# Attention values in one tile per head pair, with rows at places modulo 16

## The chip, the cores and the metric

The kernel runs on one core of one Trainium2 chip. The metric is the device time of one execution in microseconds, the median of several runs. Five engines work side by side: PE (TensorE, with its weight loads shown as PEld), DVE (VectorE), ACT (ScalarE), POOL (GpSimd) and SP (SyncE, which here only issues DMAs). Each engine takes its own instructions in order; semaphores tie them together.

## The reference

One layer of an encoder over 2048 tokens of width 1024 in float32. The tokens form a grid of 32 rows of 64. The tokens are normalised, projected to q, k, v and a gate for 16 heads of 64, and each token attends to a neighbourhood of 8 rows by 16 columns around it, with a learned bias:

```python
def row_fn(r):
    rs = jnp.clip(r - kh // 2, 0, rows - kh)          # kh = 8 key rows
    kr = lax.dynamic_slice_in_dim(kg, rs, kh, axis=1)[:, :, col_idx]
    vr = lax.dynamic_slice_in_dim(vg, rs, kh, axis=1)[:, :, col_idx]
    s = jnp.einsum('bnqhd,bknjhd->bhnqkj', qr, kr) * scale
    s = jnp.where(col_valid[None, None], s + bias[None], NEG_INF)
    p = jax.nn.softmax(s.reshape(B, H, nb, NA_QBLOCK, kh * NA_KBLOCK), axis=-1)
    o = jnp.einsum('bhnqkj,bknjhd->bnqhd', p, vr)
...
x = x + (o * jax.nn.silu(gate)) @ w_out
return rmsnorm(x, norm_f)
```

## The kernel before, in words

The first 561 us are the two projection stages (`stage_one`, `stage_two`), the last 120 us the output product and the final norm. Between them lies the attention stage, which the change touches.

Attention is done in 32 cycles. A cycle m is one entry of `order`: a pair of heads p (8 pairs; s = 0, 1 tells the two heads apart) and a frame T. A frame is 8 query rows and the key rows that they see; T = 0, 1, 2, 3 go down the grid. Cycles 0 to 15 take T = 1, then T = 0 for each pair; cycles 16 to 27 take T = 2, then T = 3 for pairs 0 to 5; cycles 28 to 31 are (6, 2), (7, 2), (7, 3), (6, 3). So a pair has a first run (T = 1 or 2) and a second run (T = 0 or 3) that share the key tile `KT`.

A frame's queries are cut in two halves of 4 rows, and its 64 columns in two quads of 4 groups of 8 columns. `HALF_ROWS[T][half]` says at which row of the frame a half's keys begin and how many rows they are (8 or 11). `FRAME[T]` is the grid row at which the frame begins, `TALL` the number of rows that the values' tile holds, 15. A tile `X[quad, half, s]` has 3 blocks of 8 columns for each of these rows, 3 x 8 x 15 = 360 elements per partition.

The loop body for cycle m runs, in program order:

- `begin(m)`: puts the coming loads on a list that is worked off while PE counts on (`later_loads`): the gate of cycle m-1, bias, queries and keys of cycle m+1 (`load_bias`, `load_q`, `load_k`) and the values of cycle m (`load_v`, L1265). All of them are issued by SP's queue, in order.
- feeds of other PE work, some 13.5 products of 128x512 (about 3 us): the last projections (L384 to L388) at first, output products (L1614 to L1618) later. Their weights and rows are split in two parts on ACT and DVE (`consume` with L185/L186 or L190/L191, `split_og` with L1455/L1456) before the turns.
- `normalise` of the quad left over from the cycle before: a reciprocal of the sums on DVE (L1357) and the scaling of X, by POOL (L1362) except for quad 1, half 1, which ACT (L1364, s = 1) and DVE (L1366, s = 0) scale.
- `turns(m-1)`: 48 transposes (L1382) of `8 * TALL` columns of X into six PSUM banks, copied to `pta` by ACT (L1389) and DVE (L1387), three copies each. Then `clear_x` has POOL zero those rows of X that the next frame does not write (L1316).
- `scores(2m)` and `scores(2m+1)`: 64 products (L1331), on DVE the sum with the bias and its minimum (L1342), on ACT the exponential with its sum (L1350), one per quad, half and s: 8 in a cycle.
- `values(m-1)`: 36 products (L1407) over `8 * TALL` partitions of `pta` and the values' tile; the product with the gate (L1413); its store (L1416).

The values of cycle m come as one DMA of 15 rows (120 partitions of 4 KB) into a tile of its own; the pool `vp` has two buffers. The keys of a first run come as one DMA (15 rows and 8 columns, or 16 rows), and those of a second run as one DMA of four rows into the same tile.

Of the kernel before, what the change touches and what calls it, by code (L numbers as in the profile page):

```python
# [11 lines left out]
F32 = mybir.dt.float32  # L12
# [3 lines left out]
AF = mybir.ActivationFunctionType  # L16
OP = mybir.AluOpType
# [44 lines left out]
def build(ctx, tc, x, xr, xt, wg, bias, w_out, n0, nf, out):  # L62
# [1167 lines left out]
            tc.add_manual_dep(d.ins, marks[at].ins.name, mybir.DependencyInfo(mybir.DependencyClass.Sync, mybir.DependencyReason.DATA),  # L1230
                              reason="loads spread over the run")

    def load_k(p, T):
        r0, r1, more = PARTS[T]
        base = 12 * (T > 1)
        a, b = r0 * GW, r1 * GW + more
        must(*[("k", p, c) for c in range(a // 512, (b + 511) // 512)])

        def keys():
            if T in (1, 2):  # L1240
# [3 lines left out]
            if T == 2:  # L1244
                nc.gpsimd.memset(t[:, 1280:1288], 0.0)
            not_until(nc.sync.dma_start(t[:, a - base * GW:b - base * GW], kd[p][:, a:b]), "values")

        return keys

    def load_q(p, T):  # L1250
        must(("q", p, T))

        def queries():
            QT[p, T] = qp([128, 512], F32, "q")
            nc.sync.dma_start(QT[p, T], qd[p][T])

        return queries

    def load_v(p, T):
        r0, r1 = FRAME[T], FRAME[T] + TALL  # L1260
        must(*[("v", p // 4, t) for t in range(r0 // 2, (r1 + 1) // 2)])
        rows = vd[p // 4][p % 4][r0 * 8192:r1 * 8192].rearrange("(k x) -> k x", x=1024)
        t = vp([128, 1024], F32, "vt")
        VT[p, T] = t.rearrange("p (s d) -> p s d", s=8)
        nc.sync.dma_start(t[:8 * TALL], rows)  # L1265

    def load_sg(p, T):
        must(("g", p, T))
# [27 lines left out]
    def make_x():  # L1296
        for half in range(2):
            for quad in range(2):
                for s in range(2):
                    X[quad, half, s] = t = xp([128, 512], F32, f"x{s}")[:, :24 * TALL]  # L1300
                    nc.gpsimd.memset(t, 0.0)
            t = ep([128, 528], F32, "sums")
            nc.gpsimd.memset(t, -NEG)
            sums.extend((t[:, :264], t[:, 264:]))
            held[half] = HALF_ROWS[order[0][1]][half]

    def clear_x(T):
        stale = []
        for half in range(2):
            (u0, n0), (u1, n1) = held[half], HALF_ROWS[T][half]  # L1310
            held[half] = u1, n1
            stale += [(half, a, b - a) for a, b in ((u0, min(u0 + n0, u1)), (max(u0, u1 + n1), u0 + n0)) if a < b]
        for quad in range(2):
            for half, a, n in stale:
                for s in range(2):
                    nc.gpsimd.memset(by_strip(X[quad, half, s], (a, n)), 0.0)  # L1316

    def scores(i, between=None):
        p, T, quad = pairs[i]
        kt, qt = KT[p, T // 2], QT[p, T]  # L1320
        both = [bank(512, f"s{s}") for s in range(2)]
        places = {}
        for half, (u, n) in enumerate(HALF_ROWS[T]):
            for s in range(2):
                places[half, s] = both[s][:, 256 * half:256 * half + WIDE * n]
            for h in range(4):
                g = 4 * quad + h
                for s in range(2):
                    a = slice(s * 64, s * 64 + 64)
                    o = (FRAME[T] + u - 12 * (T > 1)) * GW + 8 * FIRST[g]  # L1330
                    product = nc.tensor.matmul(places[half, s][h * 32:h * 32 + 32], qt[a, g * 64 + half * 32:g * 64 + half * 32 + 32],  # L1331
                                               kt[a, o:o + n * GW].rearrange("p (r c) -> p r c", c=GW)[:, :, :WIDE],
                                               start=True, stop=True, skip_group_check=True)
        if quad == 0:
            marks["scored"] = product
        ST[i] = st = tiny.tile([128, 12], F32, name="st")
        for half, (u, n) in enumerate(HALF_ROWS[T]):
            table = EM[p, T // 2, kinds_of[T][half]][quad]
            rows = [t[:, :24 * n].rearrange("p (r c) -> p r c", c=24) for t in sums[2 * half:2 * half + 2]]
            for s in range(2):  # L1340
                o = 2 * half + s
                nc.vector.tensor_tensor_reduce(rows[s][:, :, :WIDE], places[half, s].rearrange("p (r c) -> p r c", c=WIDE),  # L1342
                                               table[s].rearrange("p (r c) -> p r c", c=WIDE), -1.0, 1e38,
                                               OP.add, OP.min, st[:, o:o + 1])
            if between and half == 0:
                between()
            for s in range(2):
                o = 2 * half + s
                to = by_strip(X[quad, half, s], HALF_ROWS[T][half]).rearrange("p b (r c) -> p b r c", c=8)
                nc.scalar.activation(to, rows[s].rearrange("p r (b c) -> p b r c", b=3), AF.Exp, bias=st[:, o:o + 1], scale=-1.0,  # L1350
                                     accum_out=st[:, 4 + o:5 + o])

    def normalise(i, half):
        st = ST[i]
        _, T, quad = pairs[i]
        o = 2 * half
        nc.vector.reciprocal(st[:, 8 + o:10 + o], st[:, 4 + o:6 + o])  # L1357
        for s in range(2):
            f = st[:, 8 + o + s:9 + o + s]
            t = by_strip(X[quad, half, s], HALF_ROWS[T][half])  # L1360
            if quad == 0 or half == 0:
                nc.gpsimd.tensor_scalar(t, t, f, 1.0, op0=OP.mult, op1=OP.mult)  # L1362
            elif s:
                nc.scalar.activation(t, t, AF.Copy, scale=f)  # L1364
            else:
                nc.vector.tensor_scalar(t, t, f, None, op0=OP.mult)  # L1366
# [27 lines left out]
    def values(m):  # L1394
        p, T = order[m]
        k = 8 * TALL
        o = bank(512, "o")
        vt = VT[p, T]
# [12 lines left out]
        del VT[p, T]  # L1411
        og = ev([128, 512], F32, "og")
        nc.vector.tensor_tensor(og, o, SG.pop((p, T)), OP.mult)  # L1413

# [403 lines left out]
    def begin(m):  # L1818
# [113 lines left out]
```

## Time and profile before

| | |
|---|---|
| median of 3 runs | 992.08 us (988.28 to 993.48) |
| the profiled execution: time, span | 992.66 us, 990.9 us |
| granted PE clock, mean | 0.997 |
| busy: PE, PEld, DVE, ACT, POOL | 979.0, 796.7, 753.9, 531.9, 161.2 us |
| attention stage | 561 to 869 us of the span |
| moved by DMA | 227.95 MB |
| issues of values, of keys | 32, 32 |
| DMA to landing, values (480 KB), median | 5.9 us |

A timeline row gives start and length of a stretch in us, the engine and line, the operation, out<-in by the program's names, shapes, how many instructions were merged, and in brackets how long the engine idled before and what it waited for. A row of the groups gives count, busy us, mean ns of one, and the idle time before them with what ended it. "Issue" is idle time for which the profile shows no reason.

### The profile page before, as it was taken

What the parts mean: (1) busy time and instruction counts of PE and PEld (TensorE: products, weight loads), DVE (VectorE), ACT (ScalarE), POOL (GpSimd) and SP (SyncE); (2) the same over time, 40 slices, a digit from 0 to 9 for tenths busy, and PEclk for the clock granted to TensorE, in tenths of its full rate; (3) what the DMA queues carried; (4) which work ended last, traced back from release to release, by engine and by line L of the source; (5) the groups of instructions that cost most, each with busy time, mean ns of one, the idle gap of its engine ahead of it and who ended that gap; (6) DMA issues with size and microseconds to landing.
All of it is one profiled execution on the core that took longest, in us unless ns stands there. A gap on an engine that the chain in (4) does not pass through costs nothing.

```text
span 990.9 us, 22736 instructions
## 1 busy us (share of the span) xinstructions
PE 979.0 (99%) x8172; PEld 796.7 (80%) x8172; DVE 753.9 (76%) x1735; ACT 531.9 (54%) x1310; POOL 161.2 (16%) x430
## 2 busy tenths in 40 slices
PE   9999999999999999999999999999999999999996
PEld 6888888888888888888888778777778787888885
DVE  6899888988565876766775677768868888877865
ACT  7873245465535342343433477678768777653442
POOL 0000001231100000000001134334343343312110
PEclk9999999999999999999999999999999999999998
DMA  8943548777957836657465799988989988797753
GB/s 294 327 133 101 197 128 256 248 243 248 374 156 225 279 112 200 193 181 228 161 182 196 245 296 292 270 243 258 310 271 293 284 243 264 235 381 195 213 141 108
DMA packets 149970, 227.95 MB, mean 230 GB/s; under 512 B 13536, under 2 KB 66016, under 8 KB 149856
## 3 DMA queue, kind: packets, MB, share of 16 engines
q1 hardware_dynamic: 146832, 221.37, 70.9%
q0 software_dynamic: 2592, 4.72, 2.8%
q8 instruction: 65, 1.06, 0.4%
q14 instruction: 49, 0.40, 0.1%
q10 hardware_dynamic: 432, 0.40, 0.1%
HBM read 160.37 MB, written 66.06 MB: 229 GB/s over the span
## 4 chain that ended last, share of the span: by engine, by line
PE 98%; DMA 0%; issue 0%; ACT 0%; DVE 0%; ACTq 0%
PE pp L446 40%; PE pv L612 13%; PE py L1709 12%; PE o L1407 8%; PE s L1331 6%; PE ph L1382 5%; PE pp L388 2%; PE pp L384 2%; PE pp L386 2%; PE pv L727 2%; PE po L1618 2%; PE po L1614 2%; PE po L1616 2%; DMA raw<-in_wg_dram 0%; PE prb L235 0%
## 5 line engine op out<-in xcount | busy, mean ns | idle before, releaser
L446 PE MATMUL pp<-h,f 128*128 128x512 f32 x576 | 185.3, 389 | 0.0
L446 PE MATMUL pp<-t,f 128*128 128x512 f32 x702 | 171.3, 389 | 0.0
L446 PEld LDWEIGHTS pp<-t,f 128*128 128x128 f32 x702 | 131.8, 188 | 27.3
L1350 ACT ACTIVATE x<-sums,st 128x264 f32<-128x264 f32 (+1 forms) x256 | 124.5, 488 | 30.0 <-DVE st L1342 30.0
L446 PEld LDWEIGHTS pp<-h,f 128*128 128x128 f32 x576 | 108.1, 188 | 22.6
L446 PE MATMUL pp<-l,f 128*128 128x512 f32 x288 | 112.0, 389 | 0.0
L1362 POOL TENSOR_SCALAR x<-x,st 128x264 f32<-128x264 f32 (+1 forms) x192 | 89.0, 480 | 111.2 <-DVE st L1357 91.5
L1342 DVE CUSTOM_DVE_ANT_0 sums<-s,em 128x253 f32<-128x253 f32 (+1 forms) x256 | 91.1, 401 | 5.7 <-ACT x L1350 1.2
L429 DVE TENSOR_TENSOR f<-raw,f 128x512 fp32r<-128x512 f32 x105 | 75.9, 727 | 20.0 <-ACT f L428 19.8
L1407 PEld LDWEIGHTS o<-pta,vt 120*64 120x64 f32 x1152 | 69.9, 137 | 21.9 <-issue 15.1
L1407 PE MATMUL o<-pta,vt 120*64 120x192 f32 (+2 forms) x1152 | 84.6, 300 | 2.9 <-issue 2.9
L428 ACT ACTIVATE f<-raw 128x512 fp32r<-128x512 f32 x105 | 63.6, 622 | 36.6 <-DVE raw L435 22.0
L1387 DVE COPY pta<-ph 120x512 f32<-120x512 f32 x96 | 60.4, 684 | 16.5 <-PE ph L1382 16.3
L1389 ACT ACTIVATE pta<-ph 120x512 f32<-120x512 f32 x96 | 50.5, 599 | 35.9 <-PE ph L1382 35.9
L446 PEld LDWEIGHTS pp<-l,f 128*128 128x128 f32 x288 | 54.1, 188 | 11.2
L1331 PE MATMUL s<-kt,q 64*32 64x253 f32 (+1 forms) x2048 | 59.1, 362 | 0.0
L1382 PEld LDWEIGHTS ph<-ident,x 64*120 64x120 f32 x1536 | 47.6, 135 | 11.3 <-issue 10.6
L612 PE MATMUL pv<-wh,t 128*128 128x512 f32 x176 | 56.2, 389 | 0.0
L1709 PE MATMUL py<-woh,f 128*128 128x512 f32 x168 | 55.4, 390 | 0.0
L467 POOL TENSOR_TENSOR tmp<-tmp,rb 128x512 f32<-128x512 f32 x18 | 29.3, 1632 | 156.9 <-DVE tmp L464 141.1
L446 PE MATMUL pp<-sixths,f 128*128 128x512 f32 x198 | 52.7, 389 | 0.0
L1382 PE MATMUL ph<-ident,x 64*120 64x64 f32 x1536 | 52.0, 221 | 0.0
(231 smaller groups left out, 1888.3 us busy)
## 6 DMA issues: line engine op xcount, KB each, us to landing
raw<-in_wg_dram SPq DMA_DIRECT2D x124, 256.0 KB, 4.8
vt<-vd SPq DMA_DIRECT2D x32, 480.0 KB, 5.9
row<-in_xr_dram SPq DMA_DIRECT2D x32, 256.0 KB, 5.7
vd<-v SPq DMA_DIRECT2D x32, 256.0 KB, 3.3
sgd<-sg SPq DMA_DIRECT2D x32, 256.0 KB, 3.8
q<-qd SPq DMA_DIRECT2D x32, 256.0 KB, 4.0
sgt<-sgd SPq DMA_DIRECT2D x32, 256.0 KB, 4.7
ogd<-og SPq DMA_DIRECT2D x32, 256.0 KB, 5.9
```

Of the source, the lines that this page charges most:

```text
L428: nc.scalar.activation(t[:, 0], src, AF.Copy)
L429: nc.vector.tensor_tensor(t[:, 1], src, t[:, 0].bitcast(F32), OP.subtract)
L446: nc.tensor.matmul(B[n, P], t[:, int(m == 2), c], x[k][int(m == 1)], start=P in (1, 6, 5) and k == 0 and m == 0, stop=k == 3 and m == 2, s ...
L612: nc.tensor.matmul(p, a[:, o], b, start=P in (1, 6, 5) and k == 0 and m == 0, stop=k == 3 and m == 2, skip_group_check=True)
L1331: product = nc.tensor.matmul(places[half, s][h * 32:h * 32 + 32], qt[a, g * 64 + half * 32:g * 64 + half * 32 + 32], kt[a, o:o + n * GW].r ...
L1342: nc.vector.tensor_tensor_reduce(rows[s][:, :, :WIDE], places[half, s].rearrange("p (r c) -> p r c", c=WIDE), table[s].rearrange("p (r c) ...
L1350: nc.scalar.activation(to, rows[s].rearrange("p r (b c) -> p b r c", b=3), AF.Exp, bias=st[:, o:o + 1], scale=-1.0, accum_out=st[:, 4 + o: ...
L1362: nc.gpsimd.tensor_scalar(t, t, f, 1.0, op0=OP.mult, op1=OP.mult)
L1382: one_turn = nc.tensor.transpose(ph[h][:k, o:o + 64], X[quad, half, s][q, at:at + k], ident[q, q])
L1387: nc.vector.tensor_copy(o, i_)
L1407: product = nc.tensor.matmul(o[s * 64:s * 64 + 64, g0 * 64:g1 * 64], vt[:k, strip, s * 64:s * 64 + 64], moving, start=strip == 0, stop=str ...
L1709: nc.tensor.matmul(B[m, P], t[:, a, c], b, start=P in (1, 6, 5) and k == 0 and i == 0, stop=k == 3 and i == 2, skip_group_check=True)
```

## The change

`TALL` becomes 16, and a row r of the grid lies at place r modulo 16 in X, in `pta` and in the values' tile. The two runs of a pair share one values' tile: the first run's 16 rows are loaded as 12 and 4, the 12 one cycle earlier; the second run loads the four rows that differ over those that have become free (rows 0 to 3 for T = 0, 28 to 31 for T = 3), one cycle ahead of their use. The last four cycles, whose pairs cross, have exceptions. The keys of a first run come in two parts, the first 8 rows one cycle earlier.

Because of the modulus a half's rows may lie in two stretches: half 1 of T = 1 (places 8 to 15 and 0 to 2) and half 0 of T = 2 (places 12 to 15 and 0 to 6). There `scores` issues two exponentials instead of one, `normalise` adds the two sums on DVE and scales all 384 elements of the tile. `clear_x` works on sets of places. Turns and values span 128 columns and partitions instead of 120.

```diff
-FRAME, TALL = [0, 4, 12, 17], 15
+FRAME, TALL = [0, 4, 12, 17], 16
...
-    def load_k(p, T):
+    def load_k(p, T, part=None):
         r0, r1, more = PARTS[T]
         base = 12 * (T > 1)
-        a, b = r0 * GW, r1 * GW + more
+        first, last = part in (None, 0), part in (None, 1)
+        a = r0 * GW if first else (r0 + 8) * GW
+        b = r1 * GW + more if last else (r0 + 8) * GW
...
+    def keys_of(n):
+        (p, T), fs = order[n], []
+        if T not in (1, 2) or not in_parts(n):
+            fs.append(load_k(p, T))
+        else:
+            fs.append(load_k(p, T, 1))
+        if n + 1 < cycles and in_parts(n + 1):
+            fs.append(load_k(*order[n + 1], 0))
+        return fs
+
+    def in_parts(n):
+        return n > 1 and order[n][1] in (1, 2) and order[n - 1][1] in (0, 3)
...
-    def load_v(p, T):
-        r0, r1 = FRAME[T], FRAME[T] + TALL
+    def value_rows(n, r0, r1):
+        p, T = order[n]
         must(*[("v", p // 4, t) for t in range(r0 // 2, (r1 + 1) // 2)])
-        rows = vd[p // 4][p % 4][r0 * 8192:r1 * 8192].rearrange("(k x) -> k x", x=1024)
-        t = vp([128, 1024], F32, "vt")
-        VT[p, T] = t.rearrange("p (s d) -> p s d", s=8)
-        nc.sync.dma_start(t[:8 * TALL], rows)
+        o = r0 % TALL * 8
+        nc.sync.dma_start(VT[n][o:o + 8 * (r1 - r0)], vd[p // 4][p % 4][r0 * 8192:r1 * 8192].rearrange("(k x) -> k x", x=1024))
+
+    def first_values(n):
+        VT[n] = vp([128, 1024], F32, "vt")
+        value_rows(n, *{1: (4, 16), 2: (16, 28), 3: (16, 32)}[order[n][1]])
+
+    def load_values(m):
+        fs = []
+        if m and m - 1 < cycles - 1 and order[m - 1][1] in (0, 3):
+            VT[m - 1] = VT[m - 2]
+            fs.append(lambda: value_rows(m - 1, *((0, 4) if order[m - 1][1] == 0 else (28, 32))))
+        if m < cycles and order[m][1] in (1, 2):
+            if not in_parts(m):
+                fs.append(lambda: first_values(m))
+            fs.append(lambda: value_rows(m, *((16, 20) if order[m][1] == 1 else (12, 16))))
+        if m == cycles - 1:
+            fs.append(lambda: first_values(m))
+        elif m + 1 < cycles and in_parts(m + 1):
+            fs.append(lambda: first_values(m + 1))
+        return fs
...
+    def places_of(T, half):
+        u, n = HALF_ROWS[T][half]
+        return [(FRAME[T] + u + r) % TALL for r in range(n)]
+
+    def stretches(rows):
+        rows = list(rows)
+        cuts = [0] + [i for i in range(1, len(rows)) if rows[i] != rows[i - 1] + 1] + [len(rows)]
+        return [(a, rows[a], b - a) for a, b in zip(cuts, cuts[1:]) if a < b]
...
         stale = []
         for half in range(2):
-            (u0, n0), (u1, n1) = held[half], HALF_ROWS[T][half]
-            held[half] = u1, n1
-            stale += [(half, a, b - a) for a, b in ((u0, min(u0 + n0, u1)), (max(u0, u1 + n1), u0 + n0)) if a < b]
+            now_held = set(places_of(T, half))
+            stale += [(half, a, n) for _, a, n in stretches(sorted(held[half] - now_held))]
+            held[half] = now_held
...
-                to = by_strip(X[quad, half, s], HALF_ROWS[T][half]).rearrange("p b (r c) -> p b r c", c=8)
-                nc.scalar.activation(to, rows[s].rearrange("p r (b c) -> p b r c", b=3), AF.Exp, bias=st[:, o:o + 1], scale=-1.0,
-                                     accum_out=st[:, 4 + o:5 + o])
+                for k, (a, at, n_) in enumerate(stretches(places_of(T, half))):
+                    to = by_strip(X[quad, half, s], (at, n_)).rearrange("p b (r c) -> p b r c", c=8)
+                    e = 12 + s if k else 4 + o
+                    nc.scalar.activation(to, rows[s][:, a:a + n_].rearrange("p r (b c) -> p b r c", b=3), AF.Exp, bias=st[:, o:o + 1], scale=-1.0,
+                                         accum_out=st[:, e:e + 1])
...
+        places = stretches(places_of(T, half))
+        if len(places) > 1:
+            nc.vector.tensor_tensor(st[:, 4 + o:6 + o], st[:, 4 + o:6 + o], st[:, 12:14], OP.add)
         nc.vector.reciprocal(st[:, 8 + o:10 + o], st[:, 4 + o:6 + o])
         for s in range(2):
             f = st[:, 8 + o + s:9 + o + s]
-            t = by_strip(X[quad, half, s], HALF_ROWS[T][half])
+            t = X[quad, half, s] if len(places) > 1 else by_strip(X[quad, half, s], places[0][1:])
...
-            fs += [load_q(*nx), load_k(*nx)]
-        if m < cycles:
-            fs.append(lambda: load_v(*order[m]))
+            fs += [load_q(*nx), *keys_of(m + 1)]
+        fs += load_values(m)
```

More of the change, by code (lines that the diff above doesn't have):

```diff
@@ L1231, in not_until @@
                               reason="loads spread over the run")
-    def load_k(p, T):
+    def load_k(p, T, part=None):
         r0, r1, more = PARTS[T]
         base = 12 * (T > 1)
-        a, b = r0 * GW, r1 * GW + more
+        first, last = part in (None, 0), part in (None, 1)
+        a = r0 * GW if first else (r0 + 8) * GW
+        b = r1 * GW + more if last else (r0 + 8) * GW
         must(*[("k", p, c) for c in range(a // 512, (b + 511) // 512)])
         def keys():
-            if T in (1, 2):
+            if T in (1, 2) and first:
                 khalf.clear()
@@ L1243, in keys @@
             t = KT[p, T // 2]
-            if T == 2:
+            if T == 2 and last:
                 nc.gpsimd.memset(t[:, 1280:1288], 0.0)
@@ L1304, in make_x @@
             sums.extend((t[:, :264], t[:, 264:]))
-            held[half] = HALF_ROWS[order[0][1]][half]
+            held[half] = set(places_of(order[0][1], half))
     def clear_x(T):
@@ L1335, in scores @@
             marks["scored"] = product
-        ST[i] = st = tiny.tile([128, 12], F32, name="st")
+        ST[i] = st = tiny.tile([128, 14], F32, name="st")
         for half, (u, n) in enumerate(HALF_ROWS[T]):
@@ L1397, in values @@
         o = bank(512, "o")
-        vt = VT[p, T]
+        vt = VT[m].rearrange("p (s d) -> p s d", s=8)
         t = PT.pop(m)
```

1 line of the change is left out of this document (removed).

## The prediction

> **What bounds the kernel now.** I read the page's shares and its chain of work first, then the busy times of the attention stage alone, then the timeline of single cycles. Durations are from the profiled execution, 992.66 us with a span of 990.9 us, which stands 0.58 us above the median of the three runs, 992.08 us.
>
> ```profile
> span 990.9 us, 22736 instructions
> PE 979.0 (99%) x8172; PEld 796.7 (80%) x8172; DVE 753.9 (76%) x1735; ACT 531.9 (54%) x1310; POOL 161.2 (16%) x430
> ...
> PE 98%; DMA 0%; issue 0%; ACT 0%; DVE 0%; ACTq 0%
> ```
> ```profile
> 561.00:869.00 308.00, 305.07 (x5214) 241.60 (x5213) 242.25 (x883) 225.47 (x707) 111.01 (x378) 1.00 0.90 271
> ```
>
> PE is busy 99% of the span and is 98% of the chain. The second fence is the stage that the change touches (us of the stretch, then busy PE, PEld, DVE, ACT, POOL, granted clock, DMA share, GB/s): PE 305.07 of 308.00 us at the full clock, with the DMA engines 90% busy. So nothing can be gained there except by shorter PE work or by the 3 us in which PE idles, and what other engines lose costs nothing until PE waits for it. One cycle shows how far off such a wait is. This is cycle 12 (pair 6, frame 1), with other rows left out:
>
> ```profile
> 683.44 0.50 ACT L1350 ACTIVATE x<-sums,st 128x264 f32<-128x264 f32 x1
> ...
> 684.07 0.17 DVE L1357 RECIPROCAL st<-st 128x2 f32<-128x2 f32 x1 [0.54 <-ACT x L1350]
> 684.27 0.52 ACT L1364 ACTIVATE x<-x,st 128x264 f32<-128x264 f32 x1 [0.23 <-DVE st L1357]
> 684.34 0.48 DVE L1366 TENSOR_SCALAR x<-x,st 128x264 f32<-128x264 f32 x1
> 684.69 1.14 ACT L190 ACTIVATE woh<-raw 128x512 fp32r<-128x512 f32 x2
> 685.34 1.29 DVE L191 TENSOR_TENSOR wol<-raw,woh 128x512 fp32r<-128x512 f32 x2 [0.52 <-ACT woh L190]
> 685.82 1.49 PEld L1382 LDWEIGHTS ph<-ident,x 64*120 64x120 f32 x48 [0.35 <-issue]
> 685.82 1.62 PE L1382 MATMUL ph<-ident,x 64*120 64x64 f32 x48
> 686.54 1.58 ACT L1389 ACTIVATE pta<-ph 120x512 f32<-120x512 f32 x3 [0.71 <-PE ph L1382]
> 686.58 1.89 DVE L1387 COPY pta<-ph 120x512 f32<-120x512 f32 x3
> ...
> 687.38 1.71 PE L1331 MATMUL s<-kt,q 64*32 64x184 f32 x64
> ...
> 689.01 0.66 PE L1407 MATMUL o<-pta,vt 120*64 120x128 f32 x8
> ```
>
> The last exponential ends at 683.94. Behind it hang the reciprocal, the scaling of the probabilities (L1364 on ACT, L1366 on DVE), the weight split in the same queues (L190, L191), the turns on PE (L1382, from 685.82), their copies out of PSUM (L1389, L1387) and the values (L1407). Two margins are to be read. The last scaling ends at 684.82 and is first needed by the 13th of 48 turns, 12 x 1.49 / 48 = 0.37 us after 685.82: 1.4 us. DVE's copies end at 688.47 and the values begin at 689.01: 0.54 us.
>
> **The change part by part.** Prices by operation, from the groups by shape:
>
> ```profile
> L1350 ACT ACTIVATE x<-sums,st 128x264 f32<-128x264 f32 x192 | 96.3, 503 | 23.6 <-DVE st L1342 23.6
> L1350 ACT ACTIVATE x<-sums,st 128x192 f32<-128x192 f32 x64 | 28.3, 442 | 6.4 <-DVE st L1342 6.4
> L1357 DVE RECIPROCAL st<-st 128x2 f32<-128x2 f32 x128 | 20.2, 160 | 11.7 <-ACT x L1350 11.7
> L1364 ACT ACTIVATE x<-x,st 128x264 f32<-128x264 f32 x24 | 12.3, 514 | 5.3 <-DVE st L1357 5.3
> L1364 ACT ACTIVATE x<-x,st 128x192 f32<-128x192 f32 x8 | 3.6, 454 | 3.9 <-DVE st L1357 3.9
> L1362 POOL TENSOR_SCALAR x<-x,st 128x264 f32<-128x264 f32 x144 | 69.4, 497 | 91.5 <-DVE st L1357 91.5
> L1362 POOL TENSOR_SCALAR x<-x,st 128x192 f32<-128x192 f32 x48 | 19.9, 428 | 19.7 <-ACT x L1350 19.6
> L1316 POOL MEMSET x<- 128x72 f32 (+1 forms) x176 | 20.1, 166 | 75.7 <-PE ph L1382 75.2 <-POOL x L1316 0.5
> L1382 PE MATMUL ph<-ident,x 64*120 64x64 f32 x1536 | 52.0, 221 | 0.0
> L1382 PEld LDWEIGHTS ph<-ident,x 64*120 64x120 f32 x1536 | 47.6, 135 | 11.3 <-issue 10.6
> L1407 PEld LDWEIGHTS o<-pta,vt 120*64 120x64 f32 x1152 | 69.9, 137 | 21.9 <-issue 15.1 <-ACT x L1350 0.4 <-ACT pta L1389 0.4
> ```
>
> *Cut exponentials.* With row r at place r modulo 16, frame 1's half 1 (rows 8 to 18) and frame 2's half 0 (rows 12 to 22) wrap, the others do not. These are cycles 0, 2, ..., 28 and 29: 16 cycles, in each of which 2 quads x 2 heads exponentials become two, 64 more in all. 72 elements fewer save 503 - 442 = 61 ns, so one of 72 costs about 442 - 102 = 340 ns, and 192 + 72 cost 442 + 340 - 503 = 0.28 us more than 264 (96 + 168 the same, the price being a straight line). Exponentials follow each other without a gap, so the last of a cut cycle ends 4 x 0.28 = 1.12 us later. For frame 1 the sum of the two parts (a DVE operation on 128x2, taken at the reciprocal's 0.16 us) and the longer scaling over all 384 places (120 elements more, 0.10 us by L1364's two rows) are added: 1.38 us. For frame 2 those fall on half 0, which POOL scales, and the last scaling is 1.12 us late.
>
> *What that delay does.* In cycle 12 the last scaling ends 684.82 + 1.38 = 686.20, against 686.19 needed: the turns just hold. L190 and L191 move with it; L191 ends at 688.01 instead of 686.63, DVE's three copies follow it and end 1.89 us later at 689.90, and the values wait 0.89 us past 689.01. Behind the waiting values stand the next feed of projections and everything else on PE, so this is lost outright. Other cut cycles, with the turns' start and the values 3.19 us behind it as in cycle 12 (689.01 - 685.82):
>
> ```profile
> 611.81 0.69 DVE L186 TENSOR_TENSOR w<-raw,w 128x512 fp32r<-128x512 f32 x1 [0.66 <-ACT w L185]
> ...
> 612.16 0.96 PEld L1382 LDWEIGHTS ph<-ident,x 64*120 64x120 f32 x30 [0.35 <-issue]
> ...
> 647.71 0.47 DVE L1366 TENSOR_SCALAR x<-x,st 128x264 f32<-128x264 f32 x1
> ...
> 648.73 0.90 PEld L1382 LDWEIGHTS ph<-ident,x 64*120 64x120 f32 x27 [0.35 <-issue]
> ...
> 779.27 1.29 DVE L191 TENSOR_TENSOR wol<-raw,woh 128x512 fp32r<-128x512 f32 x2 [0.87 <-ACT woh L190]
> ...
> 779.54 0.84 PEld L1382 LDWEIGHTS ph<-ident,x 64*120 64x120 f32 x26 [0.35 <-issue]
> ```
>
> Cycle 22 (frame 2, two splits): L191 ends 780.56 + 1.12 = 781.68, the copies 783.57, values due 782.73: 0.84 us. Cycle 4 (one split): 612.50 + 1.38 + 1.89 = 615.77 against 615.35: 0.42 us. Cycle 8 (no split, little feed behind the exponentials): scaling 648.18 + 1.38 = 649.56 against 648.73 + 0.37 = 649.10: 0.46 us. So: cycles with two splits ahead of the turns (12, 14, 22, and 20 taken at 0.5) 3.1 us; with one item late on DVE (4, 6, 24, 26, 29) 5 x 0.4 = 2.0 us; cycle 8 and cycle 0 (0.3) 0.8 us; 2, 10, 16, 18 and 28 none, their queues having room. Sum 5.9 us. Bounds: nothing, if the queues' idle time takes it all; 16 x 1.38 = 22 us, if none does. I stay near the rows of single cycles.
>
> *Turns with 128 columns instead of 120* (and products over 128 rows instead of 120). A load of 64 columns takes 137 ns and one of 120 takes 135, so 8 columns more show nothing: 0. Upper end: the 48 loads of a cycle take 1.49 us, and if they set the pace, 8/120 of it for 32 cycles is 3.2 us. Lower end: the scores (L1331 in the fence of cycle 12) run 64 products in 1.71 us, 26.7 ns each against 1.62 / 48 = 33.8; at that pace the turns would gain 10.9 us.
>
> The Trainium skill, "TensorE: Matmul & The Clock Gate", section "LDWEIGHTS (loading the stationary operand)", has a load's time proportional to its columns, columns / 1.2 ns. By that, 8 columns are 6.7 ns, 10.2 us over 1536 loads if none were hidden, and the sum would be 1009. The trace does not agree in this kernel: 120 columns load no slower than 64.
>
> *POOL.* Clears go from 176 to 256 (0.166 us each), and 48 scalings grow from 264 to 384 elements (0.115 us each by L1362's two rows), some 19 us on an engine busy 16%. The clears run behind the turns while PE scores and DVE reduces; quad 0 is cleared first, and its exponentials come first. A scaling of half 0 that ends 0.2 us later is still needed only by the ninth turn. 0, at most 1 us.
>
> *Loads.* Values go from 32 issues of 480 KB (15 rows of 32 KB, 15.4 MB) to 48 (20 rows for each of 15 pairs, 32 for the one whose second run comes last, 10.6 MB), 4.7 MB less, keys go from 32 issues to 46. SP issues 30 more, about 1 per cycle; the release each waits for (the values two cycles back) is the one that L1265 waits for now. The new hazard: the four rows of a second run are loaded one cycle ahead, not two.
>
> ```profile
> 582.66 0.34 SPq L1265 DMA_DIRECT2D vt<-vd  x1
> ...
> 586.70 2.07 PE L1407 MATMUL o<-pta,vt 120*64 120x128 f32 x28
> ...
> kt<-kd SPq DMA_DIRECT2D x16, 128.0 KB, 3.9
> ```
> ```profile
> 727.69 2.56 PE L1407 MATMUL o<-pta,vt 120*64 120x128 f32 x34 [1.45 <-issue]
> ```
>
> The tightest is cycle 1: that issue slot at 582.66, values at 586.70, 4.0 us; a load of the same 128 KB takes 3.9 in the median. I take 0.4 us (0 to 3). Elsewhere the distance is about 6.5 us. Fewer bytes buy nothing: PE's idle time inside the stage, such as the 1.45 us of the last row, is put down to nothing that the profile shows, not to data. I leave it as it is (up to 3 us either way, if its place shifts).
>
> Sum: 992.66 + 5.9 + 0 + 0 + 0.4 = 999.0 us, 0.7% above the median.
>
> **The rivals.**
>
> *The cover holds (not slower).* The mechanism: the values need DVE's copies later than I charge, and the cut costs less than the straight line says. The first products of the values read columns that ACT's copies wrote (done at 688.12), DVE's are first read some four products on, 0.3 us. And queues with the idle time of cycle 12 (0.54 us before the copies' wait) absorb a delay of up to 0.5 us; that is 0.12 us for each cut instead of 0.28. From there down nothing is lost: 993. For it: PE's own waits for ACT and POOL at L1382 and L1407 are under 1 us in all now. Against: ACT's exponentials have no gaps, and cycle 12's DVE goes from L191 straight to the copies.
>
> *The turns run faster.* 128 columns is the full width, and the pace falls to that of the scores: 999.0 - 10.9 = 988, and with the cover holding 982, the only way to faster. Against: loads of 64 and 120 columns do not differ.
>
> *The loads set the turns' pace:* 999.0 + 3.2 = 1002. For it: PEld is busy 1.49 of the 1.62 us.
>
> *The late four rows:* 999.0 + 3 = 1002, if that part lands behind the rest of the queue. For it: DMA at 90%.
>
> **How the numbers follow.** Forecast 0.50 (996 to 1002), the loads' pace 0.08, late rows 0.05, cover holds 0.29 (992 to 995), faster turns 0.08. A measurement here tells about 0.5% from no change: slower begins at 997.0, faster ends at 987.1. Slower: the first three hold 0.63, less the part of the forecast that lies under 997, 0.08: 0.55. Faster: the faster turns, nearly always with some of the cover: 0.07. Same: the rest, 0.38. The time is 999.0; the range takes in the cover holding and both rivals at 1002, and leaves out the faster turns: 991 to 1004.
>
> **What would show it.** Exponentials 256 to 320, with ACT busy about 18 us more. PE waiting at the values for the copies, 0.4 to 0.9 us in cycles 4, 6, 12, 14, 20, 22, 24, with the longer waits where two splits stand ahead of the turns; at the turns in cycle 8. The turns' loads at 135 ns and 48 in 1.62 us. MB moved down by 4.7. Wrong it is if a cut exponential costs the ACT queue well under 0.28 us, if PE's idle time in the stage stays at 3 us, or if the turns' 1.62 us moves.

## The result and the profile after

The changed kernel takes 997.83 us (median of 4 runs, 997.35 to 998.95), the kernel before 991.61 us beside it: a ratio of 1.0068, interval 1.005 to 1.0086. The forecast was 999.0 us. The time came out close to the sum, but three of its terms were off, and PE waited in other places than forecast.

The page of the changed kernel, the rows that answer to the first fence of before (span, busy times, chain by engine):

```profile
span 996.1 us, 23138 instructions
...
PE 986.6 (99%) x8172; PEld 801.9 (81%) x8172; DVE 759.8 (76%) x1767; ACT 549.4 (55%) x1438; POOL 180.7 (18%) x510
...
PE 93%; DVE 2%; ACT 2%; issue 1%; DMA 1%; POOL 0%; SPq 0%; POOLq 0%; ACTq 0%; DVEq 0%
```

The span is 5.2 us longer. ACT is busy 17.5 us more (forecast: about 18), and the chain, which was PE for 98%, now runs for a few per cent through ACT and DVE. PE itself is busy 7.6 us more for the same 8172 products. What it does longer, and where it stands, shows best in a single cycle. This is cycle 12 again (pair 6, frame 1), the cycle shown before, other rows left out:

```profile
687.72 0.34 ACT L1393 ACTIVATE x<-sums,st 128x72 f32<-128x72 f32 x1
...
688.19 0.42 DVE L1402 TENSOR_TENSOR st<-st 128x2 f32<-128x2 f32 x1 [1.14 <-ACT x L1393]
688.55 0.45 PEld L1428 LDWEIGHTS ph<-ident,x 64*128 64x128 f32 x12 [0.35 <-POOL x L1408]
...
688.65 0.17 DVE L1403 RECIPROCAL st<-st 128x2 f32<-128x2 f32 x1
...
688.93 0.62 ACT L1410 ACTIVATE x<-x,st 128x384 f32<-128x384 f32 x1 [0.77 <-DVE st L1403]
...
689.49 1.38 PE L1428 MATMUL ph<-ident,x 64*128 64x64 f32 x36 [0.35 <-DVE x L1412]
690.10 1.29 DVE L191 TENSOR_TENSOR wol<-raw,woh 128x512 fp32r<-128x512 f32 x2 [0.76 <-ACT woh L190]
...
691.12 0.49 PEld L1372 LDWEIGHTS s<-kt,q 64*32 64x32 f32 x30 [0.19 <-ACT pta L1435]
691.31 1.88 DVE L1433 COPY pta<-ph 128x512 f32<-128x512 f32 x3
...
692.05 0.50 PEld L1372 LDWEIGHTS s<-kt,q 64*32 64x32 f32 x32 [0.44 <-DVE pta L1433]
...
692.95 1.08 PEld L1453 LDWEIGHTS o<-pta,vt 128*64 128x64 f32 x20 [0.41 <-issue]
```

The last exponential ends at 688.06, 0.49 us ahead of the turns' start at 688.55; before it ended 1.88 us ahead. The sum of the two parts (L1402), the reciprocal and the scaling follow, and the scaling ends at 689.55. The turns do 12 and then stand until 689.46, where the forecast had them "just hold". Then the scores stand twice, for copies out of PSUM (`pta`): all PSUM tiles of this kernel come from one pool of eight banks, and the banks that the scores write are those that the turns' copies set free. The values begin at 692.95, 0.24 us before DVE's last copy ends (691.31 + 1.88), and wait for nothing. From the turns' start to the values' start it is 4.40 us, against 3.19 before.

That distance, the start of the turns to the start of the values, is the measure used below. In the kernel before it is 3.19 us after the turns of most first runs and 3.42 after the others. With 128 columns and no cut it is 3.27 and 3.50 (experiment `a_uncut`). What the changed kernel has beyond that is its wait, cycle by cycle, in us:

| cycle | 0 | 2 | 4 | 6 | 8 | 10 | 12 | 14 | 18 | 20 | 22 | 23 | 24 | 29 | others | sum |
|---|---|---|---|---|---|---|---|---|---|---|---|---|---|---|---|---|
| forecast | 0.3 | 0 | 0.4 | 0.4 | 0.5 | 0 | 0.9 | 0.9 | 0 | 0.5 | 0.8 | 0 | 0.4 | 0.4 | 0.4 (26) | 5.9 |
| measured | 0.69 | 0.57 | 0.33 | 0.29 | 0.78 | 0.66 | 1.13 | 0.99 | 0.28 | 0.51 | 0.26 | 0.13 | 0.65 | 0.41 | 0 | 7.7 |

About 4.9 us of the 7.7 lie inside the turns and 2.8 in the scores behind them. The names behind the arrows, of what ended a wait, have to be read with care here: the 0.35 us ahead of the turns in cycle 12 is put down to POOL, but every unhindered cycle has the same 0.35 us there, put down to issue. What counts is the idle time as a whole.

The groups by shape of the changed kernel (busy us, mean ns of one, idle time before):

```profile
L1393 ACT ACTIVATE x<-sums,st 128x264 f32<-128x264 f32 x128 | 64.3, 503 | 18.0 <-DVE st L1383 18.0
L1393 ACT ACTIVATE x<-sums,st 128x192 f32<-128x192 f32 x96 | 42.4, 442 | 9.2 <-DVE st L1383 9.2
...
L1393 ACT ACTIVATE x<-sums,st 128x72 f32<-128x72 f32 x32 | 10.9, 341 | 0.0
...
L1402 DVE TENSOR_TENSOR st<-st 128x2 f32<-128x2 f32 x32 | 8.8, 275 | 10.9 <-ACT x L1393 10.9
...
L1383 DVE CUSTOM_DVE_ANT_0 sums<-s,em 128x253 f32<-128x253 f32 x192 | 74.1, 418 | 10.9 <-ACT x L1393 8.0 <-POOL x L1357 0.2
...
L1428 PEld LDWEIGHTS ph<-ident,x 64*128 64x128 f32 x1536 | 51.8, 138 | 14.4 <-issue 9.9 <-POOL x L1408 3.3 <-POOL kt L1247 1.0
...
L1372 PEld LDWEIGHTS s<-kt,q 64*32 64x32 f32 x2048 | 37.7, 106 | 11.7 <-DVE pta L1433 1.5 <-ACT pta L1435 1.3 <-issue 0.7
...
L1428 PE MATMUL ph<-ident,x 64*128 64x64 f32 x1536 | 57.5, 226 | 1.8 <-DVE x L1412 1.1 <-POOL kt L1247 0.4
```

Two of these rows in the kernel before, the sums with the bias and the scores' loads:

```profile
L1342 DVE CUSTOM_DVE_ANT_0 sums<-s,em 128x253 f32<-128x253 f32 x192 | 73.1, 419 | 5.1 <-ACT x L1350 1.2 <-issue 0.9
...
L1331 PEld LDWEIGHTS s<-kt,q 64*32 64x32 f32 x2048 | 37.2, 106 | 9.9 <-issue 1.1
```

An exponential of 72 elements takes 341 ns, where the straight line said 340. The turns' loads take 138 ns instead of 135 and stand idle 14.4 us, 3.1 more than the 11.3 of before. The turns' products are busy 5.5 us more (52.0 before) and idle 1.8 us; these 7.3 us are the 4.9 of waits and a slower pace, on which more below. The scores' loads now name the copies among what they wait for. And DVE's sums with the bias now wait 8.0 us for exponentials (1.2 before), as ACT has fallen behind DVE.

### The profile page after: what moved, and what is told of

The parts are those of the page before. It is cut to its first block, busy times and chain, and to the rows that moved or that the text cites. A ratio compares the mean times of both kernels' runs of the same rounds, so it can differ in the third digit from the quotient of the medians.

```text
span 996.1 us, 23138 instructions
## 1 busy us (share of the span) xinstructions
PE 986.6 (99%) x8172; PEld 801.9 (81%) x8172; DVE 759.8 (76%) x1767; ACT 549.4 (55%) x1438; POOL 180.7 (18%) x510
## 4 chain that ended last, share of the span: by engine, by line
PE 93%; DVE 2%; ACT 2%; issue 1%; DMA 1%; POOL 0%; SPq 0%; POOLq 0%; ACTq 0%; DVEq 0%
PE pp L446 40%; PE pv L612 13%; PE py L1754 12%; PE o L1453 6%; PE s L1372 5%; PE ph L1428 5%; PE pv L727 2%; PE pp L384 2%; PE pp L386 2%; ACT x L1393 2%; PE pp L388 2%; PE po L1659 1%; PE po L1663 1%; PE po L1661 1%; DVE sums L1383 1%
## 5 line engine op out<-in xcount | busy, mean ns | idle before, releaser
L1393 ACT ACTIVATE x<-sums,st 128x192 f32<-128x192 f32 (+2 forms) x320 | 142.3, 446 | 36.3 <-DVE st L1383 36.2
L1408 POOL TENSOR_SCALAR x<-x,st 128x264 f32<-128x264 f32 (+2 forms) x192 | 92.7, 500 | 113.8 <-DVE st L1403 85.1
L1453 PEld LDWEIGHTS o<-pta,vt 128*64 128x64 f32 x1152 | 70.0, 137 | 18.1 <-issue 11.7
L1453 PE MATMUL o<-pta,vt 128*64 128x192 f32 (+2 forms) x1152 | 83.8, 299 | 0.0
L1433 DVE COPY pta<-ph 128x512 f32<-128x512 f32 x96 | 60.2, 683 | 6.7 <-PE ph L1428 6.5
L1428 PEld LDWEIGHTS ph<-ident,x 64*128 64x128 f32 x1536 | 51.8, 138 | 14.4 <-issue 9.9
L1435 ACT ACTIVATE pta<-ph 128x512 f32<-128x512 f32 x96 | 50.5, 594 | 18.5 <-PE ph L1428 18.3
L1393 ACT ACTIVATION_READ_ACCUMULATOR x<-sums,st 128x1 f32 x320 | 59.9, 187 | 0.0
L1428 PE MATMUL ph<-ident,x 64*128 64x64 f32 x1536 | 57.5, 226 | 1.8 <-DVE x L1412 1.1
L1342 POOL MEMSET x<- 128x384 f32 x8 | 3.4, 420 | 299.0 <-DVE f L429 260.6
```

The lines of the kernel that those rows point to most:

```text
L1393: nc.scalar.activation(to, rows[s][:, a:a + n_].rearrange("p r (b c) -> p b r c", b=3), AF.Exp, bias=st[:, o:o + 1], scale=-1.0, accum_out ...
L1428: one_turn = nc.tensor.transpose(ph[h][:k, o:o + 64], X[quad, half, s][q, at:at + k], ident[q, q])
L1433: nc.vector.tensor_copy(o, i_)
L1453: product = nc.tensor.matmul(o[s * 64:s * 64 + 64, g0 * 64:g1 * 64], vt[:k, strip, s * 64:s * 64 + 64], moving, start=strip == 0, stop=str ...
```

## Experiments

Two theories stood after the result. A: the cut exponentials delay the scaling, PE waits for it, and that is the whole loss. B: the new loads (values in two pieces, keys in two parts, more issues) are what costs, and the cut is covered. The first three kernels each do one part of the change; times are medians, with the ratio to the kernel before and its interval.

**The change without the cut (`a_uncut`).** Modulus, loads, 128 columns and clears stay; a half that wraps is written in one piece from place 0 on, so that its rows lie at wrong places and the result is not that of the reference; the second exponential, the sum of two parts and the longer scaling are left out.

```diff
-                for k, (a, at, n_) in enumerate(stretches(places_of(T, half))):
+                for k, (a, at, n_) in enumerate(uncut(T, half)):    # [(0, 0, n)] where it wraps
...
-        places = stretches(places_of(T, half))
+        places = uncut(T, half)
```

> The changed kernel, but a half whose rows wrap gets one exponential over 11 rows, written to places 0 to 10, and its scaling covers those (so these rows lie at wrong places in the tile: the time is that of the change without the cut). Theory A (the cut exponentials make PE wait: 4.8 us at the turns, 2.6 us for PSUM banks at the scores): both waits go, the turns keep 31.5 ns each (1.48 us from first to last), time 989 to 994 us. Theory B (the new loads and their order make PE wait, the cut is covered): 996 to 998 us, waits stay.

990.88 us against 991.53 for the kernel before, ratio 0.9989 (0.9978 to 1.0000); the changed kernel is 6.95 us above it. The waits are gone: by the groups by shape the idle time of the turns' loads is 11.3 us, as in the kernel before, and that of the scores' 9.6 us; the turns' products are busy 54.4 us, 2.4 above the kernel before.

```profile
L1432 PEld LDWEIGHTS ph<-ident,x 64*128 64x128 f32 x1536 | 50.0, 138 | 11.3 <-issue 10.6 <-POOL x L1412 0.7
...
L1376 PEld LDWEIGHTS s<-kt,q 64*32 64x32 f32 x2048 | 36.9, 106 | 9.6 <-issue 0.7
...
L1432 PE MATMUL ph<-ident,x 64*128 64x64 f32 x1536 | 54.4, 224 | 0.0
```

The cut, with the sum and the longer scaling that come with it, is the whole loss: A holds, and B would have left some 7 us here.

**The cut alone (`b_cut`).** The kernel before, with the same halves cut at the same rows, the sum of two parts and the longer scaling; 15 rows, 120 columns and the old loads stay.

```diff
+    CUT = {(1, 1): 8, (2, 0): 4}
...
-                nc.scalar.activation(to, rows[s]..., accum_out=st[:, 4 + o:5 + o])
+                cut = CUT.get((T, half), n)
+                for k, (a, n_) in enumerate([(0, cut), (cut, n - cut)][:1 + (cut < n)]):
+                    nc.scalar.activation(to, rows[s][:, a:a + n_]..., accum_out=st[:, e:e + 1])
...
+        if (T, half) in CUT:
+            nc.vector.tensor_tensor(st[:, 4 + o:6 + o], st[:, 4 + o:6 + o], st[:, 12:14], OP.add)
-            t = by_strip(X[quad, half, s], HALF_ROWS[T][half])
+            t = X[quad, half, s] if (T, half) in CUT else by_strip(...)
```

> The kernel before with nothing but the cut: half 1 of frame 1 in 8 and 3 rows, half 0 of frame 2 in 4 and 7, the two sums added, the scaling over the whole tile. Loads, 15 rows and 120 columns as before. Theory A: PE waits at the turns and at the scores as in the changed kernel, about 7.4 us in all, time 995 to 1000 us (the upper half if the 4.2 us of gaps put down to issue stay). Theory B: 990 to 993 us.

998.63 us, ratio 1.0059 (1.0037 to 1.0080): 7.1 us, the same loss from the other side (7.6 us by the distance from turns to values), with the same idle time ahead of the turns (14.6 us) and the same waits for copies in the scores:

```profile
L1389 PEld LDWEIGHTS ph<-ident,x 64*120 64x120 f32 x1536 | 49.2, 135 | 14.6 <-issue 9.6 <-POOL x L1369 3.9 <-POOL kt L1245 0.8
...
L1333 PEld LDWEIGHTS s<-kt,q 64*32 64x32 f32 x2048 | 37.0, 106 | 13.3 <-DVE pta L1394 1.9 <-issue 1.6 <-ACT pta L1396 1.2
```

**The old kernel with 16 rows (`b_tall16`).** 128 columns and partitions, one load of 512 KB per cycle, no modulus.

```diff
-FRAME, TALL = [0, 4, 12, 17], 15
-HALF_ROWS = [..., [(3, 11), (7, 8)]]
+FRAME, TALL = [0, 4, 12, 16], 16
+HALF_ROWS = [..., [(4, 11), (8, 8)]]
```

> The kernel before with tiles of 16 rows (frame 3 begins at row 16), no modulus, loads of 512 KB: the turns have 128 columns, nothing is cut. If the turns' pace follows the columns: 48 turns in 1.48 us from first to last start instead of 1.41, 2.3 us in all, 994 us (990 to 995, since gaps put down to issue may move). If the slower turns of the changed kernel come from its waits: 1.41 us and 990 to 993 us.

990.96 us, ratio 0.9992 (0.9979 to 1.0005). Beside `a_uncut` (990.88) it differs in the loads and in where the rows lie, and moves 5.9 MB more (229.00 against 223.09): the new loads give and cost nothing that stands out of the noise of about 1 us. The stage in both, `b_tall16` first (us, busy PE, PEld, DVE, ACT, POOL, granted clock, DMA share, GB/s):

```profile
561.00:869.00 308.00, 308.00 (x5223) 245.33 (x5222) 245.03 (x888) 228.06 (x712) 113.91 (x402) 1.00 0.89 278
```
```profile
561.00:869.00 308.00, 308.00 (x5223) 245.39 (x5223) 244.95 (x886) 227.33 (x710) 127.23 (x458) 1.00 0.84 258
```

PE has no idle time in either, with the DMA engines busy 89% and 84%. It had 2.9 us in the kernel before, so wider turns cost less than their own price; more on this below.

**The modulus without the cut, rows in place (`a_fold`).** Blocks of X lie 160 elements apart from element 32 on, a wrapping half is written in one exponential that runs past the block's end, and the scaling, in two pieces, puts the rest in its place.

```diff
-                for k, (a, at, n_) in enumerate(stretches(places_of(T, half))):
-                    ... two exponentials, two sums
+                to = by_strip(X[quad, half, s], (starts_at(T, half), n))...    # places 8 to 18, or -4 to 6
+                nc.scalar.activation(to, rows[s]..., accum_out=st[:, 4 + o:5 + o])
...
+            for a, at, n in places:
+                t = by_strip(X[quad, half, s], (at, n))
+                t0 = by_strip(X[quad, half, s], (starts_at(T, half) + a, n))
...
-            at = (2 - b) * k
+            at = (2 - b) * 160 + 32
```

> The changed kernel with the wrap moved from the exponentials to the scaling: blocks of X are 20 places apart, an exponential writes its 11 rows in one piece past the end (frame 1) or ahead of the beginning (frame 2) of the 16 places, and the scaling, in two pieces, puts the rows that stick out at their places. Exponentials 256 instead of 320; for three of four wrapped scalings the second piece is on POOL. Theory A: the waits at the turns and banks go but for 0 to 1 us, time 989 to 994 us. Theory B: 996 to 998 us.

991.87 us, ratio 1.0005 (0.9990 to 1.0021), 1.0 us above `a_uncut`. Its waits beyond those of `a_uncut` come to 1.2 us, in cycles 0 (0.2), 1 (0.2) and 29 (0.9), and the turns of every cycle take 0.01 us longer. In cycle 29 POOL's pieces are late, and the turns stand 0.56 us for them; the other two are not traced. So the modulus itself costs nothing clear of the noise as long as ACT's row of exponentials isn't lengthened.

**Half of the cut (`b_cut_one`).** As `b_cut`, for one of the two heads only: 32 more exponentials instead of 64. If every cut cost its share, half of 7 us would be left; if there is a margin to use up first, less.

```diff
-                cut = CUT.get((T, half), n)
+                cut = n if s else CUT.get((T, half), n)
```

> The kernel before with half the cut: of the two heads only head 0 gets two exponentials in the wrapped halves (2 more per cycle of the 16, 32 in all); one sum is added, the scaling covers the whole tile. The delay of the last scaling is 0.56 + 0.16 + 0.10 us in frame 1 and 0.56 in frame 2. Theory A (PE waits only for what exceeds each cycle's margin, 0.9 to 1.4 us at the turns): waits at the turns under 0.5 us in all, at the scores under 0.7, time 991 to 993 us. Theory P (the loss is in proportion to the ACT time added): half of the full cut's 7.1 us, 995 us.

992.4 us against 990.91, ratio 1.0009 (0.9993 to 1.0025). The margin takes it: the turns' loads idle no longer than in the kernel before, 11.3 us, though part of it is put down to POOL.

```profile
L1389 PEld LDWEIGHTS ph<-ident,x 64*120 64x120 f32 x1536 | 47.7, 135 | 11.3 <-issue 8.8 <-POOL x L1369 1.4 <-POOL kt L1245 1.1
...
L1333 PEld LDWEIGHTS s<-kt,q 64*32 64x32 f32 x2048 | 37.2, 106 | 12.2 <-issue 2.7 <-ACT pta L1396 0.3 <-DVE pta L1394 0.2
```

By the turns-to-values distance one cycle (0, 0.4 us) waits for the cut. The scores' excess is for the most part one pause of 1.96 us in cycle 20 that no other engine ends. Half of 7.1 us on 990.91 would have been a ratio of 1.0036, above the interval. And as this kernel has the scaling over the whole tile, and the sum for its one cut head, these alone are not what costs the 7 us.

**Fewer columns (`b_short`).** Frames 0 and 3 need only 12 key rows. The kernel before, with 96 columns and partitions for these (16 of the 32 cycles) and loads of 12 rows.

```diff
+FRAME, TALL, ROWS_OF = [0, 4, 12, 20], 15, [12, 15, 15, 12]
+HALF_ROWS = [..., [(0, 11), (4, 8)]]
...
-        k = 8 * TALL
+        k = 8 * ROWS_OF[T]
```

> The kernel before, with the turns, their copies, the values and the values' load over 12 rows (96 columns and partitions) in frames 0 and 3, which need no more, and 15 rows in frames 1 and 2. If the turns' pace follows the columns (30.0 ns at 120, 31.4 at 128: 0.18 ns a column), 48 turns of 96 columns take some 1.20 us from first to last start instead of 1.41, 16 cycles gain 3.3 us: 988.2 us. If only 128 columns are slow: 1.41 us in all cycles and 990 to 993 us.

988.4 us (12 runs) against 990.91, ratio 0.9974 (0.9959 to 0.9989): the one kernel here that beats both. The turns by shape:

```profile
L1382 PEld LDWEIGHTS ph<-ident,x 64*120 64x120 f32 x768 | 23.8, 135 | 5.6 <-issue 4.9 <-POOL x L1362 0.7
L1382 PEld LDWEIGHTS ph<-ident,x 64*96 64x96 f32 x768 | 22.4, 123 | 5.6 <-issue 5.6
```

A load of 96 columns takes 123 ns, and 48 turns without a wait take, first start to last, 1.33 us with 96 columns, 1.41 with 120 and 1.48 with 128. So the pace is no straight line of the columns: 24 fewer take off 0.08 us, 8 more add 0.07. The gain in the turns is 16 x 0.08 = 1.3 us, less than half of what was expected; it lies inside the interval (1.1 to 4.1 us), and the rest of the 2.5 us isn't traced to a row.

**Where PE pauses for nothing (`b_shift`, `b_again`).** The kernel before loses 4.3 us of the stage in pauses put down to issue, and the profiles with 128 columns lose between nothing and 1.0 us. `b_again` is the kernel before unchanged; `b_shift` runs 64 more transposes ahead of the stage, so that every later instruction of PE has a number 128 higher (a load and a product each; 131 by the records, in which three of PE's sequencer are added).

```diff
     stage_two()
+    both = [bank(512, f"ph{h}") for h in range(2)]
+    for i in range(64):
+        ...
+        nc.tensor.transpose(both[h][:120, ...], ident[q, :120], ident[q, q])
```

> The kernel before once more, for a second profile. If the gaps put down to issue are a matter of the single execution, they come at the same instructions with other lengths, or fail to come; the copies' and turns' margins stay as they were.

> The kernel before with 64 more transposes of a constant (some 2 us of PE, 128 PE instructions) between the projections and the attention stage; nothing reads them. The gaps put down to issue in the values and scores (4.2 us in the profile before, at PE instructions whose numbers differ by multiples of 256). If they sit where blocks of 256 instructions begin, they move by 128 instructions to other places of other cycles, or go; time 989 to 995 us. If they hang on the loads of those cycles, they stay in cycles 1, 9, 16 and 26 and the time is 993.5 us.

Times: `b_shift` 991.63, ratio 1.0012 (0.9992 to 1.0031); `b_again` 991.32 (one run). PE's loads after a pause of over half a microsecond, in `b_again` and then in `b_shift`:

```profile
590.13 0.52 PEld L1407 LDWEIGHTS o<-pta,vt 120*64 120x64 f32 x8 [1.85 <-issue]
...
626.86 1.82 PEld L1407 LDWEIGHTS o<-pta,vt 120*64 120x64 f32 x23 [1.31 <-issue]
```
```profile
645.63 2.37 PEld L1407 LDWEIGHTS o<-pta,vt 120*64 120x64 f32 x34 [0.65 <-issue]
...
739.42 0.52 PEld L1407 LDWEIGHTS o<-pta,vt 120*64 120x64 f32 x6 [0.71 <-issue]
```

The extra transposes moved the pauses to other cycles and left 1.9 us of them. Counted through the records of PE, its loads and its sequencer, the first instruction behind such a pause is 5825, 10689 and 14017 in the kernel before (and 8385 for the shorter one of cycle 9), 5825, 7105, 10689 and 14017 in `b_again` and 7873 and 11201 in `b_shift`: each of these numbers is 193 modulo 256, and a transfer of 16 KB on the queue that the page calls "instruction" begins 2.2 to 2.5 us ahead of each. The page of the kernel before has that queue with 65 packets and 1.06 MB, some 16 KB each:

```profile
q8 instruction: 65, 1.06, 0.4%
```

Blocks of 256 begin at other places as well, and most cost nothing. Taking transfers and blocks in order, one for one, the records tell them apart: of the 40 such places inside the stage, in the kernel before and again in `b_again`, the four with a pause are those whose transfer began less than 2.5 us ahead; at the other 36 it began 2.7 us or more ahead. In some other profiles the border is less sharp (in `b_cut` 2.3 us once without a pause and 2.65 once with one). So what PE waited for there was most likely its own instructions: the block's transfer had begun too late. Which blocks are late differs from one execution to the next.

**Traffic against those pauses (`a_uncut_traffic`).** `a_uncut` with one more DMA per cycle, between two places in memory, 16.8 MB read and written in all, to see whether the pauses come with the load on the memory.

```diff
+        if m < cycles:
+            fs.append(lambda: nc.sync.dma_start(junk[m], xr[m * 64:m * 64 + 64, :]))
```

> The uncut version of the changed kernel (rows at wrong places, as before) with one DMA more per cycle that copies 256 KB of an input to a place nobody reads: 8.4 MB read and as much written, more than the 4.7 MB that the change saves. Theory S (the smaller loads took the gaps put down to issue away): gaps of 2 to 4 us come back in the values and scores and the time is 992 to 995 us. Theory C (they went by the chance of where a block of 256 instructions begins within a cycle): no gap, 990 to 992 us.

992.41 us (990.5 to 995.67), ratio 1.0006 (0.9987 to 1.0024); the profiled execution (span 988.7 us, as `a_uncut`) has one pause, of 0.73 us, 0.32 more than the 0.41 that stands ahead of these values in any case. The median is 1.5 us above that of `a_uncut` and its runs spread more, but the two intervals of the ratio overlap. Inconclusive.

**Once more (`a_again`, `a_uncut_again`, `b_tall16_again`).** The same kernels again, one profile each, to see whether the waits repeat.

> The changed kernel once more. Waits at the turns 4.8 us and at the scores 2.7 us as in its first profile, within 0.3 us, since they follow from the order of the work; gaps put down to issue under 1 us if the kernel has none, 1 to 4 us if the first profile was one execution's luck.

> The uncut version once more, for a second profile. If it is the kernel that has no gaps put down to issue: none here either, span within 1 us of 988.7. If it was the single execution: gaps of 1 to 4 us.

> The 16-row version of the kernel before once more. Its loads are larger than those of the kernel before, and its first profile had no gap put down to issue. If gaps hang on the bytes: 1 to 4 us of them here, span 989 to 992. If on where blocks of instructions begin: none, 988.

996.99, 989.52 and 990.39 us. The wait of the changed kernel came out at 7.8 us (7.7 at first), at the same cycles within 0.05 us each; without the cut it was under 0.2 us again; and neither `a_uncut_again` nor `b_tall16_again` had a pause over half a microsecond. `b_tall16_again` lost 1.0 us in three shorter ones, at instructions 5825, 8385 and 14017, whose transfers began 2.2 to 2.4 us ahead.

## Why the prediction was right, step by step

*The price of a cut exponential:* right. In a cycle of frame 1, the exponentials of 192 and 72 elements that replace one of 264 take 503 to 442 + 341 ns; 0.28 us each, 17.5 us on ACT in all.

*The delay of the last scaling (1.38 us for frame 1, 1.12 for frame 2):* too small. Measured against the turns' start, it ends 1.6 us later in cycle 4 and 2.00 us later in cycle 12. In cycle 12 the exponentials give 1.39 us of it (1.88 - 0.49) instead of 1.12, and the tail behind them 0.6 instead of 0.26: from 683.94 to 684.82 it was 0.88 us, from 688.06 to 689.55 it is 1.49. L1402, taken at 0.16 us, takes 0.42 where it has waited for ACT (0.275 in the mean). Frame 2 was held to be late by 1.12 us on POOL, in time for the turns. It was not, in cycles 18, 24 and 29. Cycle 24:

```profile
802.64 1.22 POOL L1408 TENSOR_SCALAR x<-x,st 128x384 f32<-128x384 f32 x2 [0.40 <-DVE st L1403]
...
803.00 0.42 PEld L1428 LDWEIGHTS ph<-ident,x 64*128 64x128 f32 x10 [0.35 <-issue]
...
803.91 1.30 PEld L1428 LDWEIGHTS ph<-ident,x 64*128 64x128 f32 x38 [0.50 <-POOL kt L1247]
```

POOL's scaling of half 0 ends at 803.86, the turns do 10 and go on at 803.91.

*Where PE waits:* the step that failed. The forecast had PE wait at the values for DVE's copies, in cycle 8 alone at the turns. It waits at the turns, for the scaling, and at the scores, whose PSUM banks those copies free. That second wait is nowhere in the prediction: it looked for the reader of `pta`, not for the next writer of `ph`'s banks. The values wait for nothing, as the first rival ("the values need DVE's copies later than I charge") had it; the rest of that rival, 993, fell. `b_cut_one` shows its idea of a margin to be right up to half of the cut. What it cited in its favour, waits for ACT and POOL at L1382 and L1407 "under 1 us in all", is 1.5 us by the groups by shape (0.7 for POOL, 0.4 twice for ACT); nothing in the sum rests on it.

*How much:* 5.9 us forecast, 7.7 measured in the trace, 6.95 and 7.1 in the two pairs of medians. Of the five cycles held to have room, 16 and 28 had it. Cycles 2 and 10 wait 1.2 us together: their room was lent by a pause of PE in the cycle ahead of them, 1.45 us in cycle 1 and 0.5 in cycle 9 of the kernel before, during which ACT and DVE ran on. The pauses are gone in the changed kernel and the room with them. In `b_cut`, which has the pauses (1.54 and 0.90 us), cycles 2 and 10 do not wait.

*Turns at 128 columns:* forecast 0, between -10.9 and +3.2. In `a_uncut` it is 32 x (1.479 - 1.408) = +2.3 us, first start to last. The row of cycle 12 there, 1.62 us in the kernel before:

```profile
685.44 1.70 PE L1432 MATMUL ph<-ident,x 64*128 64x64 f32 x48
```

The prediction had named a move of this 1.62 as a sign of being wrong, and for this term it was: that loads of 64 and of 120 columns take the same did not mean that "8 columns more show nothing". The loads' pace, a rival at 3.2, fits best, at seven tenths of its price. The Trainium skill, "TensorE: Matmul & The Clock Gate", section "LDWEIGHTS (loading the stationary operand)", would have had 10.2 us, an estimate from its time proportional to the columns. The trace does not agree with that size (1.5 ns a turn for 8 columns, not 6.7), though the sign was right.

*POOL and the late four rows:* forecast 0 and 0.4 us; the second is 0. In cycle 1, the tightest, the values start 3.50 us after the turns (584.44), as in cycles without such a load:

```profile
587.94 2.38 PEld L1453 LDWEIGHTS o<-pta,vt 128*64 128x64 f32 x36 [0.41 <-issue]
```

*Pauses put down to issue, left as they were, up to 3 us either way:* some 4.3 us of them went, more than the 3 allowed for (1.45, 0.5, 1.8 and 0.5 us in cycles 1, 9, 16 and 26).

So in the profiled executions 7.7 + 2.3 - 4.3 = +5.7 us stand against 5.9 us between the turns of cycle 0 and those of cycle 31; the rest of the span is 0.7 us shorter, which makes the 5.2. The forecast's 5.9 + 0.4 = 6.3 stand against the 6.2 us between the medians. The -4.3 belongs to one execution: by the medians everything but the cut comes to -0.65 us (`a_uncut` against the kernel before), and as the turns cost 2.3 of it, the pauses are worth about -3 us on average, an estimate that rests on these two numbers. The forecast was right in its mechanism (the cut exponentials, through the scaling, onto PE) and in the size of its main term to within a quarter. That the sum came out to a microsecond is luck: a term that was put at nothing (the turns, 2.3), one that was short (the waits, by 1 to 2) and one that was left as it was (the pauses, some -3 to -4.3) nearly cancel.

## What to carry to other kernels

An engine that is busy half the time can still be a row of work without gaps just ahead of the bound one: count what an edit adds to that row between its last input and the first consumer, and compare it with the margin there. Here half of the cut stayed inside the margin and cost nothing clear of the noise; the whole of it cost 7 us. When copies out of PSUM come late, look for the next writer of their banks, not only for the reader of the copy. And room that an engine has behind a pause of the bound engine is not its own: it goes when the pause goes.

## What the hardware showed beyond that

A pause of PE may cost a second time. In `b_short` one of 2.19 us ended at 590.58, and the five microseconds from there on ran at a granted clock of 0.66 (columns as in the windows above):

```profile
590.58 0.52 PEld L1407 LDWEIGHTS o<-pta,vt 96*64 96x64 f32 x8 [2.19 <-issue]
```
```profile
590.50:595.50 5.00, 4.92 (x19) 3.80 (x20) 2.12 (x5) 1.73 (x4) 0.95 (x2) 0.66 0.96 313
```

It is one case: behind the pauses of 1.85 us in `b_again` and 1.96 us in `b_cut_one` the clock stayed at 1.00, and no run here varied the pause alone.

Why the profiled executions with 128 columns and no cut (`a_uncut`, `b_tall16`, both again, `a_fold`, `a_uncut_traffic`) show at most one pause of 0.5 to 0.75 us each, and those with 120 columns one to four of 0.5 to 2.2 us, at the same count of 8172 products on PE (8236 in `b_shift`), stays open: the records show that a late transfer goes with each pause, not why it is late. Traffic alone did not bring the pauses back in the profiled execution, and a shift of the instructions moved them without removing them.
